# Hybrid recurrent, retention and FFN block: written order for three engines from the retention output to the output projection, and another order of the seven products

## The chip, the cores and the metric

The kernel runs on one core of a Trainium2 chip. TensorE (PE) multiplies, VectorE (DVE) and ScalarE (ACT) work elementwise on SBUF and PSUM, SyncE (SP) issues the loads. The metric is the device time of one execution in microseconds. Before the change it is 1084.58 us, the median of three runs (1083.65 to 1086.42).

## What is computed

One layer over 16 meta and 512 given tokens with 1024 channels. A normed input goes through one wide projection into eight parts: a gated linear recurrence, a retention with four heads of 512 value channels, and two gates. Cut to what the change touches:

```python
z = xn @ w_in[l]
u_rnn, u_gate, q, k, v, g_ret, ga, gb = jnp.split(z, IN_SPLITS, axis=-1)
...
o = retention(q, k, v.reshape(bsz, t, RET_HEADS, RET_DV))
o_b = head_rms(o).reshape(bsz, t, RET_HEADS * RET_DV) * jax.nn.silu(g_ret)

mixed = (jax.nn.sigmoid(ga) * (o_a @ w_branch_rnn[l])
         + jax.nn.sigmoid(gb) * (o_b @ w_branch_ret[l]))
h = h + mixed @ w_out[l]
```

`head_rms` divides each head's output by the root of the mean of its squares. Then come a norm, an up projection with a short convolution and a GELU gate, a down projection and a last norm. All of it is fp32.

## The kernel before

Every fp32 factor is held as two f16 halves. `split` makes them: the hi half by a scaled copy on ScalarE (L91), the lo half, what hi leaves over, on VectorE (L92), which so waits for ScalarE. A product of two such factors is three matmuls (hi hi, hi lo, lo hi; `SPLIT`).

Weights come in units of up to 1 MB, loaded into one of two raw buffers on SP's queue and split into `wt` tiles, of which there are ten. `unit_load` queues a unit's load and the steps that make its tiles; `tick` emits the next step if the tiles of all units from the current one on stay under `ahead[0]`; `get` emits all that is left of a unit.

The gate projections and the product with `w_branch_ret` use a scheme of seven block products instead of eight on 2 x 2 blocks (`fast_products`). The weight side needs the forms B11, B21, B22 and T1 to T4. `fast_steps` makes them in five steps: a tile with B11, a tile with B21 and B22, three sums on VectorE within the raw buffer (L231 to L233), and two tiles with two T forms each. The token side needs A11, A12, A22 and F3, F5, F6, F7. Each product is 12 matmuls of 257 columns (24 for `w_branch_ret`) into a PSUM bank `pa`, `pb` or `pe`. Three products add up in `pa`; between them ScalarE copies what is there into `kept` (twice) and `last` (L784), so the next product into `pa` waits for the copy. VectorE adds the banks and the copies (L801, L805, L812). The gate function then runs on ScalarE (L817), and `finish` uses the result.

The stretch in question, in the order of the code:

- `retention_out(h)`: four blocks of 24 matmuls (L864), each read twice by ScalarE (copy L868, square L870); VectorE adds the squares up (L872). `head_norm` sums over partitions (L879), takes the root (L881, with a load of ScalarE's function table) and the reciprocal (L883); `scale_head` multiplies it in (L917).
- `gated(h)` for the first three heads: two gate units, interleaved with `retention_out(h + 1)`. At the end of a unit the gate multiplies the head's output (L890), `ob_forms` forms differences d and y of it (L900 to L903) and splits four tensors into the `ob` tiles, four hi on ScalarE and four lo on VectorE.
- `values(h)` between the heads: five blocks of up to 24 matmuls (L842, L834), two to a PSUM pair, each split into `v` tiles.
- The mix stage: units with a sigmoid for `ga` and `gb` (`mix_unit`), the branch products (`branch`, `mix_first`), the two gate units of the fourth head, and `mix_products`, which ends in the `mx` tiles (L981, L987). Then the first of four output blocks, `out_proj(0)` (L1123).

Up to the end of the recurrence, the code that stands before this stretch runs in written order on PE, ACT and DVE (`manual_schedule`, closed at L647). From there on the tile framework's scheduler orders each engine's instructions by its own costs and priorities; the code sets only what depends on what.

## Time and profile before

| | |
|---|---|
| runs | 1083.65, 1084.58, 1086.42 us |
| profiled execution | 1084.11 us, span 1082.4 us |
| granted TensorE clock, mean | 0.999 |
| retention stage, with the change's first product | 290 to 437 us |
| mix stage up to the first output block | 437 to 663 us |

A span is the time from the first instruction to the last. In the views, a row of work gives its busy time, and in square brackets, or behind a second bar, the idle time of its engine just before it and what ended that. PEld is TensorE's weight load, which runs beside the matmuls. Matmuls overlap, so the distance from start to start (pitch) of a block says more than its modelled length.

### The profile page before, as it was taken

To read this page: it belongs to the slowest core of one execution; us is meant where nothing else is said; L and a number is where in the kernel's file an instruction comes from. 1 tells how busy PE (TensorE), PEld (TensorE's weight loads), DVE (VectorE), ACT (ScalarE), POOL (GpSimd) and SP (SyncE) were. 2 spreads that over 40 slices of the span, in tenths; PEclk is the share of its full clock that TensorE was granted. 3 is DMA by queue.
4 is the path that set the end of the run, shared out by engine and by line. 5 is a ranking of instruction groups with operands and counts; after the bars stand their busy time and mean duration, and the time that the engine had idled before them with its cause. 6 is when DMAs were issued, how large, how long until landed. Compare 5 with 4: busy or idle time off the path is not lost.

```text
span 1082.4 us, 20933 instructions
## 1 busy us (share of the span) xinstructions
PE 1059.8 (98%) x9026; PEld 856.8 (79%) x9026; DVE 839.8 (78%) x1220; ACT 567.8 (52%) x847; POOL 6.9 (1%) x20
## 2 busy tenths in 40 slices
PE   8999999999999999999999999999999999999997
PEld 5888888875684858888888885588888888888885
DVE  6875699998786969878697775378767776888875
ACT  6568963534564747566454453264544454454442
POOL 2000000000000000000000000000000000000000
PEclk9999999999999999999999999999999999999999
DMA  5423243431211222423333355053232323113322
GB/s 189 142 88 108 79 137 118 156 118 40 78 41 58 100 64 64 127 88 118 103 103 118 117 195 176 2 188 107 96 109 88 116 80 117 41 60 118 117 79 78
DMA packets 105814, 111.48 MB, mean 103 GB/s; under 512 B 3455, under 2 KB 97381, under 8 KB 105722
## 3 DMA queue, kind: packets, MB, share of 16 engines
q1 hardware_dynamic: 105288, 109.75, 30.9%
q8 instruction: 70, 1.15, 0.4%
q10 hardware_dynamic: 146, 0.27, 0.1%
q14 instruction: 22, 0.18, 0.1%
q0 software_dynamic: 288, 0.14, 0.0%
HBM read 108.05 MB, written 2.10 MB: 102 GB/s over the span
## 4 chain that ended last, share of the span: by engine, by line
PE 71%; DVE 17%; ACT 8%; issue 2%; DMA 1%; ACTq 0%; DVEq 0%
PE ps L370 33%; PE P L1251 9%; PE pa L779 7%; DVE wt L92 5%; PE ps L842 4%; PE pm L370 4%; PE ps L1123 3%; PE pe L779 3%; PE ps L383 2%; ACT wt L91 2%; PE pb L779 2%; PE ps L864 1%; DMA raw<-in_w_out 1%; DVE rnn L578 1%; DVE raw L231 1%
## 5 line engine op out<-in xcount | busy, mean ns | idle before, releaser
L370 PEld LDWEIGHTS <-wt 128*128 128x128 f16 x4224 | 410.7, 97 | 63.5 <-DVE t L670 1.4
L92 DVE SCALAR_TENSOR_TENSOR wt<-raw,wt 128x1024 f16<-128x1024 f32 (+2 forms) x270 | 296.6, 1112 | 73.9 <-ACT wt L91 72.0
L91 ACT ACTIVATE wt<-raw 128x1024 f16<-128x1024 f32 (+2 forms) x270 | 256.2, 964 | 163.7 <-PE ps L370 28.3
L779 PEld LDWEIGHTS <-wt 128*128 128x128 f16 x2016 | 195.2, 97 | 37.5 <-issue 10.3
L370 PE MATMUL ps<-x2h,wt 128*128 128x258 f16 x1440 | 218.9, 273 | 0.0
L370 PE MATMUL ps<-xh,wt 128*128 128x257 f16 (+2 forms) x1056 | 163.9, 275 | 1.1 <-DVE t L670 1.1
L370 PE MATMUL ps<-x2l,wt 128*128 128x258 f16 x720 | 137.8, 273 | 0.0
L1208 DVE SCALAR_TENSOR_TENSOR cv<-ps,vt,cv 128x512 f32<-128x512 f32 x96 | 72.0, 750 | 54.4 <-ACT cv L1206 53.1
L370 PE MATMUL ps<-xl,wt 128*128 128x257 f16 (+2 forms) x528 | 102.3, 275 | 0.0
L1251 PE MATMUL P<-wt,act 128*128 128x256 f16 x792 | 88.3, 273 | 0.0
L1251 PEld LDWEIGHTS <-act 128*128 128x128 f16 x792 | 77.4, 98 | 9.1
L842 PE MATMUL ps<-wt,xh 128*128 128x512 f16 x256 | 76.5, 379 | 1.2 <-DVE v L92 1.0
L779 PE MATMUL pa<-xs,wt 128*128 128x257 f16 x576 | 71.6, 273 | 4.7 <-ACT kept L784 4.4
L1206 ACT ACTIVATE cv<-ps,vt,vt 128x512 f32<-128x512 f32 x48 | 37.1, 773 | 57.1 <-PE ps L370 52.4
L370 PE MATMUL pm<-oa,wt 128*128 128x257 f16 x480 | 55.4, 274 | 0.0
L842 PEld LDWEIGHTS <-xh 128*128 128x128 f16 x256 | 24.8, 98 | 30.9 <-issue 2.9
L842 PE MATMUL ps<-wt,xl 128*128 128x512 f16 x128 | 48.5, 379 | 0.0
L779 PE MATMUL pa<-ob,wt 128*128 128x257 f16 x384 | 45.7, 274 | 2.0 <-ACT kept L784 1.4
L1123 PE MATMUL ps<-wt,mx 128*128 128x512 f16 x192 | 44.9, 379 | 1.6 <-ACT mx L91 1.1
L231 DVE TENSOR_TENSOR raw<-raw 128x1024 f32<-128x1024 f32 x35 | 42.7, 1221 | 0.6
L383 PEld LDWEIGHTS <-wt 128*128 128x128 f16 x288 | 28.4, 100 | 7.3 <-issue 1.5
L1123 PEld LDWEIGHTS <-mx 128*128 128x128 f16 x192 | 17.4, 98 | 20.4 <-ACT mx L91 1.6
(255 smaller groups left out, 1283.9 us busy)
## 6 DMA issues: line engine op xcount, KB each, us to landing
raw<-in_w_in SPq DMA_DIRECT2D x41, 1024.0 KB, 4.8
raw<-in_w_up SPq DMA_DIRECT2D x24, 1024.0 KB, 5.0
raw<-in_w_down SPq DMA_DIRECT2D x48, 256.0 KB, 3.8
raw<-in_w_branch_ret SPq DMA_DIRECT2D x16, 512.0 KB, 4.1
raw<-in_w_branch_rnn SPq DMA_DIRECT2D x8, 640.0 KB, 4.4
raw<-in_w_out SPq DMA_DIRECT2D x4, 1024.0 KB, 5.2
xin<-in_x SPq DMA_DIRECT2D x4, 512.0 KB, 5.2
h<-in_x SPq DMA_DIRECT2D x4, 512.0 KB, 5.2
```

The costliest lines, as they stand in the source:

```text
L91: nc.scalar.activation(hi, src, AF.Copy, scale=s)
L92: nc.vector.scalar_tensor_tensor(lo, src, s, hi, op0=ALU.mult, op1=ALU.subtract)
L231: nc.vector.tensor_tensor(pair, pair, rv[:, :, right].rearrange("p (h k) c -> p h k c", h=2), op=ALU.add)
L370: nc.tensor.matmul(ps[:, hf, :n], w(aw, k, col, P), src(ax, k, c0, n), start=k == 0 and (aw, ax) == (0, 0), stop=k == nk - 1 and aw == 1)
L383: nc.tensor.matmul(ps[:, hf, :n], w(aw, k, col, P), src(ax, k, c0, n), start=k == 0 and (aw, ax) == (0, 0), stop=k == KD - 1 and aw == 1)
L578: nc.vector.tensor_tensor_scan(xr, r, t, 0.0, op0=ALU.mult, op1=ALU.add)
L779: nc.tensor.matmul(ps[:, :257], ws[k // 4](wf, aw, k % 4), src(xf_, ax, k), start=first and k == 0 and (aw, ax) == (0, 0), stop=k == last_ ...
L842: nc.tensor.matmul(pb, xf(ax, k, XF + j0, nb), w(aw, k % 4, 0, 512), start=i == 0, stop=i == 23)
L1123: nc.tensor.matmul(ps[:, n], mx[k][:, a, c0:c0 + P], wo[k // 2](aw, k % 2, n * 512, 512), start=j == 0, stop=j == 23)
L1206: nc.scalar.activation(vv_, ps[:, :, 2:258], AF.Identity, scale=vt2[:, 96 + ch:97 + ch], bias=b_ff[:, ch:ch + 1])
L1208: nc.vector.scalar_tensor_tensor(vv_, ps[:, :, j:j + 256], vt2[:, 48 * j + ch:48 * j + ch + 1], vv_, op0=ALU.mult, op1=ALU.add)
L1251: nc.tensor.matmul(pd[:, 256 * tt:256 * tt + 256], t[:, ax, c0 + tt * P:c0 + tt * P + P], w(wf, aw, i), start=q % 6 == 0 and tt == 0 and i ...
```

## The change

From `retention_out(0)` to the end of `out_proj(0)`, PE, ACT and DVE take their instructions in the order in which the code emits them. The seven products run as B11, B21, T2, T3, T1, B22, T4 (before: B11, T3, T2, B21, T1, B22, T4), the tile with T4 and T2 is made ahead of the one with T1 and T3, and `last` is gone: the copy goes into `g1` itself. A weight form is made at the latest when a product asks for it (`form`), tiles are counted one by one (made, less freed, at most ten), and a step is ticked after every product. In the mix stage, the first product of `mix_products` moves ahead of the gate unit's last two, and another piece of work (`fill`: a unit's first product, a branch, or k = 0 to 3 of the first output block) stands between its sixth and its seventh. `out_proj(0)` ends with k = 4, 5, 7, 6, and its PSUM layout changes behind it. No matmul and no elementwise operation is added or left out.

```diff
@@ -232,38 +232,54 @@
-        at = {"B11": (0, 0), "B21": (1, 0), "B22": (1, bc), "T1": (2, 0), "T3": (2, bc), "T4": (3, 0), "T2": (3, bc)}
+        at = {"B11": (0, 0, 1), "B21": (1, 0, 2), "B22": (1, bc, 2), "T4": (2, 0, 4), "T2": (2, bc, 4),
+              "T1": (3, 0, 5), "T3": (3, bc, 5)}
         def form(nm, a, k):
-            i, c0 = at[nm]
+            i, c0, n = at[nm]
+            while emitted.get(u, 0) < n:
+                emit_step()
             return tiles[i][a][:, k, c0:c0 + bc]
+        u = len(loaded) - 1
         wviews.append(form)
-        return [cut(top, left), cut(low, slice(0, 2 * bc)), sums,
-                cut(top, slice(0, 2 * bc)), cut(low, slice(0, 2 * bc))]
+        return [(cut(top, left), True), (cut(low, slice(0, 2 * bc)), True), (sums, False),
+                (cut(low, slice(0, 2 * bc)), True), (cut(top, slice(0, 2 * bc)), True)]
...
     current = [0]
+    emitted, made, freed = {}, {}, {}
+    exact = [False]
...
     def emit_step():
-        u, run = steps[done[0]]
+        u, (run, new) = steps[done[0]]
         while len(loaded) < min(u + 2, len(units)):
...
         run()
+        emitted[u] = emitted.get(u, 0) + 1
+        made[u] = made.get(u, 0) + new
         done[0] += 1
+    def free(u, n=None):
+        freed[u] = made.get(u, 0) if n is None else freed.get(u, 0) + n
...
-    def get(u):
+    def start(u):
         current[0] = max(current[0], u)
...
             queue(unit_load())
+        return wviews[u]
+    def get(u):
+        start(u)
         while done[0] < len(steps) and steps[done[0]][0] <= u:
...
@@ -276,7 +292,10 @@
             u = steps[done[0]][0]
-            if sum(unit_tiles(i) for i in range(current[0], u + 1)) > ahead[0]:
+            if exact[0]:
+                if sum(made.values()) - sum(freed.values()) + steps[done[0]][1][1] > 10:
+                    return
+            elif sum(unit_tiles(i) for i in range(current[0], u + 1)) > ahead[0]:
                 return
...
@@ -783,35 +803,45 @@
-        kept, last = wtile("kept"), wtile("last")
-        g0, g1 = wtile("g0"), wtile("g1")
+        def release():
+            for u in us:
+                free(u, 1)
         h0, h1 = slice(0, 257), slice(257, TQ)
+        kept = wtile("kept")
         pa = bank("pa")
...
         keep(kept[:, h0], pa)
+        release()
+        yield
+        g0 = wtile("g0")
+        pb = bank("pb")
+        product(pb, "B21", "A12", True)
+        nc.vector.tensor_tensor(g0[:, h0], pb[:, :257], kept[:, h0], op=ALU.add)
+        yield
+        product(pa, "T2", "F6")
+        keep(kept[:, h1], pa)
         yield
...
         yield
-        product(pa, "T2", "F6")
-        keep(kept[:, h1], pa)
-        yield
-        pb = bank("pb")
-        product(pb, "B21", "A12", True)
-        nc.vector.tensor_tensor(g0[:, h0], pb[:, :257], kept[:, h0], op=ALU.add)
-        yield
         product(pa, "T1", "F5")
-        keep(last[:, h0], pa)
-        nc.vector.tensor_tensor(g1[:, h1], pe[:, :257], last[:, h0], op=ALU.add)
+        g1 = wtile("g1")
+        keep(g1[:, h0], pa)
+        nc.vector.tensor_tensor(g1[:, h1], pe[:, :257], g1[:, h0], op=ALU.add)
+        release()
         yield
...
         finish(1, g1)
+        release()
+        yield
         product(pe, "T4", "A22")
...
         finish(0, g0)
+        release()
...
@@ -921,22 +953,27 @@
             a = gate_unit(h, i)
-            next(a)
+            advance(a, 1)
             if i == 0:
                 head_norm(h)
-            for _ in range(2):
-                next(a)
-                tick()
+            advance(a, 2)
             next(other)
             scale_head(h, i)
-            for _ in range(2):
-                next(a)
-                tick()
+            advance(a, 2)
             next(other)
-            for _ in a:
-                pass
+            advance(a, 1)
+            rest(a)
         for _ in other:
...
+    def advance(run, n, each=1):
+        for _ in range(n):
+            next(run)
+            tick(each)
+    def rest(run):
+        for _ in run:
+            tick()
...
@@ -947,7 +984,10 @@
     psum_layout(acc=2, bank=4)
-    ahead[0] = 9
+    for u in range(u_v[1][1] + 1):
+        free(u)
+    exact[0] = True
+    order.enter_context(tc.manual_schedule(engines=ORDERED))
     for _ in retention_out(0):
...
@@ -989,11 +1025,13 @@
-        return fast_products(ws, ob_form, func, finish)
+        return fast_products(u_bb[2 * i:2 * i + 2], ob_form, func, finish)
...
         ps = acc("pm")
-        project(ps, get(us.pop(0)), 0, src, HH, nk)
+        u = us.pop(0)
+        project(ps, get(u), 0, src, HH, nk)
+        free(u)
         tick(2)
...
@@ -1003,19 +1041,27 @@
-    def advance(run, n):
-        for _ in range(n):
-            next(run)
-            tick()
-    def rest(run):
-        for _ in run:
-            pass
+    def out_products(i, ks, ps=None, halo=None):
+        first = ps is None
+        if first:
+            ps = acc("ps")
+        c0 = 2 + P * i
+        for n in range(2):
+            for k in ks:
+                w = get(u_out[k // 2])
+                for a, aw in SPLIT:
+                    nc.tensor.matmul(ps[:, n], mx[k][:, a, c0:c0 + P], w(aw, k % 2, n * 512, 512),
+                                     start=first and k == 0 and (a, aw) == (0, 0),
+                                     stop=k == ks[-1] and k > 5 and a == 1)
+                if halo is not None:
+                    halo_part(halo, 4 * n + k // 2, 4 * (k % 2))
+        return ps
...
             run = mix_unit(u_ga, i)
-            next(run)
+            advance(run, 1)
         advance(run, 4)
...
@@ -1033,30 +1079,33 @@
         after = mix_unit(u_ga, i + 1)
-        next(after)
+        advance(after, 1)
         rest(run)
...
-    def gate_b(i):
-        ahead[0] = 10
-        run = mix_unit(u_gb, i)
-        advance(run, 3)
-        ahead[0] = 12
-        advance(run, 2)
+    def gate_b(i, run, fill):
+        if run is None:
+            run = mix_unit(u_gb, i)
+            advance(run, 1)
+        advance(run, 4)
+        product = mix_products(i)
+        advance(product, 1, 2)
         rest(run)
-        for _ in mix_products(i):
-            tick(2)
-        tick()
-        ahead[0] = 10
-    gate_b(0)
-    gate_a(3)
-    gate_b(1)
-    mix_first(7, branch(u_ba, oa_of, NR))
-    gate_b(2)
-    gate_b(3)
+        advance(product, 4, 2)
+        after = fill()
+        rest(product)
+        return after
+    def first_of(us, i):
+        run = mix_unit(us, i)
+        advance(run, 1)
+        return run
+    gate_a(3, gate_b(0, None, lambda: first_of(u_ga, 3)))
+    mix_first(7, gate_b(1, None, lambda: branch(u_ba, oa_of, NR)))
+    first_out = gate_b(3, gate_b(2, None, lambda: first_of(u_gb, 3)), lambda: out_products(0, range(4)))
...
@@ -1110,21 +1158,9 @@
-    psum_layout(bank=2, acc=3)
-    def out_proj(i):
-        ps = acc("ps")
+    def out_proj(i, ps=None):
         halo = halo_start() if i == 1 else None
-        c0 = 2 + P * i
-        for n in range(2):
-            j = 0
-            for k in range(KD):
-                for a, aw in SPLIT:
-                    nc.tensor.matmul(ps[:, n], mx[k][:, a, c0:c0 + P], wo[k // 2](aw, k % 2, n * 512, 512),
-                                     start=j == 0, stop=j == 23)
-                    j += 1
-                if halo is not None:
-                    halo_part(halo, 4 * n + k // 2, 4 * (k % 2))
+        ps = out_products(i, (4, 5, 7, 6), ps) if ps is not None else out_products(i, range(KD), None, halo)
         hv = h2[i].rearrange("p (a b) -> p a b", a=2)
...
@@ -1136,7 +1172,10 @@
-    xns = [out_proj(0)[0]]
+    xns = [out_proj(0, first_out)[0]]
+    order.close()
+    exact[0] = False
+    psum_layout(bank=2, acc=3)
     for i in range(1, 4):
```

Two places show what this does to the engines' orders. The numbers behind the names tell buffers apart.

On ScalarE, at the crossing from the first to the second gate unit of the first head. `g0`, `g1` are gate values, `ob` and `ob11` the split outputs, `kept` the copy that the next unit's third product waits for, `wt` weight tiles. Before:

```order
L91 ACTIVATE wt_3994<-raw_3866 128x512
L91 ACTIVATE wt_4024<-raw_3866 128x1024
L817 ACTIVATE g0_3565<-g0_3565 128x514
L91 ACTIVATE ob11_3754<-or0_3441 128x257
L91 ACTIVATE ob_3757<-or0_3442 128x514
L91 ACTIVATE wt_4085<-raw_3866 128x1024
L784 ACTIVATE kept_3769<-pa_3773 128x257
L91 ACTIVATE ob_3760<-y_3749 128x514
L91 ACTIVATE ob_3763<-d_3748 128x514
L868 ACTIVATE or1_3623<-ps_3821 128x514
```

Of the changed kernel:

```order
L847 ACT_TABLE_LOAD
L847 ACTIVATE g1_3684<-pa_3563 128x257
L847 ACTIVATE g1_3684<-g1_3684 128x257
L91 ACTIVATE wt_3734<-raw_3249 128x1024
L847 ACTIVATE g0_3586<-g0_3586 128x514
L91 ACTIVATE ob11_3758<-or0_3443 128x257
L91 ACTIVATE ob_3761<-or0_3444 128x514
L91 ACTIVATE ob_3764<-y_3753 128x514
L91 ACTIVATE ob_3767<-d_3752 128x514
L804 ACTIVATE kept_3770<-pa_3771 128x257
L91 ACTIVATE wt_3787<-raw_3601 128x1024
```

`kept` stood ahead of the splits of y and d and now stands behind all four splits.

On VectorE, in the first gate unit of the second head, from the sum for `g1` (L805, now L831) to the start of the output forms. Before:

```order
L805 TENSOR_TENSOR g1_4114<-pe_4135,last_4112 128x257
L917 TENSOR_TENSOR or1_3624<-or1_3624,rt_4132 128x514
L92 SCALAR_TENSOR_TENSOR wt_4416<-raw_4348,wt_4416 128x1024
L92 SCALAR_TENSOR_TENSOR wt_4433<-raw_4348,wt_4433 128x1024
L872 TENSOR_TENSOR ssum_4173<-ssum_4173,sq_4263 128x514
L890 TENSOR_TENSOR or1_3622<-g1_4114,or1_3622 128x514
L812 TENSOR_TENSOR g0_4113<-pe_4135,kept_4111 128x257
L92 SCALAR_TENSOR_TENSOR wt_4542<-raw_4414,wt_4542 128x512
L92 SCALAR_TENSOR_TENSOR wt_4572<-raw_4414,wt_4572 128x1024
L890 TENSOR_TENSOR or1_3621<-g0_4113,or1_3621 128x514
L231 TENSOR_TENSOR raw_4414<-raw_4414 128x2x4x128
```

Of the changed kernel:

```order
L831 TENSOR_TENSOR g1_4236<-pe_4208,g1_4236 128x257
L92 SCALAR_TENSOR_TENSOR wt_4241<-raw_4091,wt_4241 128x1024
L904 TENSOR_TENSOR ssum_4178<-ssum_4178,sq_4270 128x514
L922 TENSOR_TENSOR or1_3623<-g1_4236,or1_3623 128x514
L92 SCALAR_TENSOR_TENSOR wt_4288<-raw_4091,wt_4288 128x1024
L841 TENSOR_TENSOR g0_4140<-pe_4208,kept_4116 128x257
L922 TENSOR_TENSOR or1_3622<-g0_4140,or1_3622 128x514
L932 TENSOR_TENSOR d_4306<-or1_3622,or1_3623 128x514
L933 TENSOR_TENSOR y_4307<-or1_3622 128x257
L934 TENSOR_TENSOR y_4307<-d_4306 128x257
```

The sum for `g0` (L812, now L841) came right behind the gate product of `g1`; now the lo half of a weight tile stands between them, and another one ahead of the addition of squares.

More of the change, by code (lines that the diff above doesn't have):

```diff
@@ L206, in run @@
                 split(tiles[i][:, 0, sl], tiles[i][:, 1, sl], raw[:, i * hn:(i + 1) * hn][:, sl], SW)
-            return run
+            return run, c == 0
         wviews.append(lambda a, k, c0, m: tiles[k // hk][:, a, k % hk * ncol + c0:k % hk * ncol + c0 + m])
@@ L457, in first_step @@
     def first_step():
-        steps[done[0]][1]()
+        steps[done[0]][1][0]()
         done[0] += 1
@@ L769, in x_forms, with fast_products @@
         return x_form_t[i // 2][:, 2 * (i % 2) + a, k]
-    def fast_products(ws, src, func, finish):
+    def fast_products(us, src, func, finish):
+        ws = [start(u) for u in us]
         last_k = 4 * len(ws) - 1
@@ L846, in values @@
         vv[h] = vt
+        for u in u_v[h]:
+            free(u)
     def retention_out(h):
@@ L892, in finish @@
                 ob_forms(h, i, ot[2 * i], ot[2 * i + 1])
-        return fast_products([get(u_gr[h][i])], x_forms, gate_func(AF.Silu), finish)
+        return fast_products([u_gr[h][i]], x_forms, gate_func(AF.Silu), finish)
     def ob_forms(h, i, t0, t1):
@@ L970, in mix_unit @@
     def mix_unit(us, i):
-        return fast_products([get(us[i])], x_forms, gate_func(AF.Sigmoid), lambda j, g: sig.update({2 * i + j: g[:, :TQ]}))
+        return fast_products([us[i]], x_forms, gate_func(AF.Sigmoid), lambda j, g: sig.update({2 * i + j: g[:, :TQ]}))
     def mix_products(i):
-        ua, ub = u_bb[2 * i], u_bb[2 * i + 1]
-        ws = [get(ua), get(ub)]
-        current[0] = ua
         def func(dst, src, sign, c0):
@@ L1026, in hybrid_block_kernel @@
         run = gate_unit(3, i)
-        next(run)
+        advance(run, 1)
         if i == 0:
@@ L1039, in hybrid_block_kernel @@
     mix_first(5, branch(u_ba, oa_of, NR))
-    def gate_b(i):
-        ahead[0] = 10
-        run = mix_unit(u_gb, i)
-        advance(run, 3)
-        ahead[0] = 12
-        advance(run, 2)
-        rest(run)
-        for _ in mix_products(i):
-            tick(2)
-        tick()
-        ahead[0] = 10
-    gate_b(0)
-    gate_a(3)
-    gate_b(1)
-    mix_first(7, branch(u_ba, oa_of, NR))
-    gate_b(2)
-    gate_b(3)
+    def gate_b(i, run, fill):
[5 more added lines that the diff above has]
+        advance(product, 1, 2)
+        rest(run)
+        advance(product, 4, 2)
[4 more added lines that the diff above has]
+        run = mix_unit(us, i)
+        advance(run, 1)
+        return run
+    gate_a(3, gate_b(0, None, lambda: first_of(u_ga, 3)))
+    mix_first(7, gate_b(1, None, lambda: branch(u_ba, oa_of, NR)))
+    first_out = gate_b(3, gate_b(2, None, lambda: first_of(u_gb, 3)), lambda: out_products(0, range(4)))
     x2h = xslot([P, KD, TQ], F16, "x2h")
@@ L1073, in hybrid_block_kernel @@
         nc.sync.dma_start(halo_x[a][0:2], meta[NM - 2:NM, sl])
-    wo = [get(u) for u in u_out]
     def halo_start():
```

3 lines of the change are left out of this document (2 added, 1 removed).

## The prediction

> **What bounds the kernel now.** I read the page's busy line first, then the chain that ended last, then the busy time by stage (the change touches about 290 to 663 us and nothing else), then TensorE's waits in that stretch. In the windows the columns are PE, PEld, DVE, ACT, POOL busy us, granted clock, DMA share, GB/s; in the waits, total us, times, longest.
>
> ```profile
> PE 1059.8 (98%) x9026; PEld 856.8 (79%) x9026; DVE 839.8 (78%) x1220; ACT 567.8 (52%) x847; POOL 6.9 (1%) x20
> PE 71%; DVE 17%; ACT 8%; issue 2%; DMA 1%; ACTq 0%; DVEq 0%
> ...
> 290.00:437.00 147.00, 142.46 (x1204) 105.10 (x1201) 119.90 (x178) 87.74 (x151) 0.00 (x0) 1.00 0.23 77
> 437.00:663.00 226.00, 220.87 (x1949) 189.80 (x1947) 177.92 (x238) 120.15 (x180) 0.00 (x0) 1.00 0.40 127
> ...
> PE pa L779 <- ACT kept L784: 5.8, 9, 1.4
> PE ps L1123 <- ACT mx L91: 1.1, 1, 1.1
> PE ps L842 <- DVE v L92: 1.0, 2, 0.5
> PE pa L779 <- ACT last L784: 0.5, 1, 0.5
> PE ps L1123 <- DVE mx L92: 0.5, 1, 0.5
> PE ps L879 <- DVE ssum L872: 0.2, 1, 0.2
> ```
>
> TensorE is the bound, and it hardly waits: 15 waits, 9.1 us, none over 1.4. A block of 12 matmuls has a pitch of 1.33 us and a modelled length of 1.49 (rows below), so each wait costs about 0.16 more than the view books: 9.1 + 15 x 0.16 = **11.5 us**. That is all that the change could win, 1.1% of the run. What it can lose is not bounded in this way: in the retention stage (290 to 437) VectorE is busy 119.9 of 147 us, 82%, and ScalarE 60%. There the queues of the two have little room, so the order in them matters.
>
> **The change part by part.** Work taken out or added: none. TensorE's and VectorE's instructions are the same in number and shape, `last` only becomes part of `g1`. So every microsecond of difference is a stall of TensorE that comes or goes. I put a stall as the lateness of a block's start against the sum of the pitches ahead of it.
>
> The block pitches, and how long the chain at the end of a gate unit takes, stand in the chain of waits and in the timeline about the first unit crossing:
>
> ```profile
> 301.69 1.33 PE pa L779 x12
> 303.02 1.84 PE ps L864 x24
> ...
> 316.66 0.69 DVE L900 TENSOR_TENSOR d<-or,or 128x514 f32<-128x514 f32 x1
> ...
> 317.60 0.42 DVE L902 TENSOR_TENSOR y<-d 128x257 f32<-128x257 f32 x1
> 317.80 0.37 ACT L784 ACTIVATE kept<-pa 128x257 f32<-128x257 f32 x1
> ...
> 318.07 0.62 ACT L91 ACTIVATE ob<-y 128x514 f16<-128x514 f32 x1
> 318.22 1.49 PE L779 MATMUL pa<-xs,wt 128*128 128x257 f16 x12 [0.78 <-ACT kept L784]
> ...
> 318.73 0.63 ACT L91 ACTIVATE ob<-d 128x514 f16<-128x514 f32 x1
> 319.27 0.58 ACT L868 ACTIVATE or<-ps 128x514 f32<-128x514 f32 x1
> ```
>
> T2 adds into the bank that B11 filled, so it waits until `kept` has been read out of it. Now, `kept` runs at 317.80, ahead of the two splits of y and d; the scheduler put it there because y wasn't ready. And 24 matmuls of retention (1.84 us) stand between the B11 and the T2 of the second unit. Both go. In program order `kept` stands behind all four hi splits of the unit before (the rows of ScalarE's order above), and only B21 stands between B11 and T2.
>
> The chain from L841 (the sum behind T4) to T2 then is bare of any choice. Durations:
>
> ```profile
> L890 DVE TENSOR_TENSOR or<-g,or 128x514 f32<-128x514 f32 x16 | 11.0, 688 | 0.0
> L817 ACT ACTIVATE g<-g 128x514 f32<-128x514 f32 x16 | 10.0, 625 | 3.1 <-DVE g L812 2.9
> L812 DVE TENSOR_TENSOR g<-pe,kept 128x257 f32<-128x257 f32 x20 | 8.4, 419 | 0.0
> ```
>
> Sum 0.42 + silu 0.63 + product with the gate 0.60 (next one follows at its pitch, 0.69 less the overlap of 0.09 that 316.66 + 0.61 shows for the rows of that size) and two hand-overs of 0.05 (318.02 to 318.07): 1.75 us to the start of d. From the start of d to the start of `ob<-y`: 318.07 - 316.66 = 1.41; to the next, 0.54 by 318.73 to 319.27; to `kept` another 0.54; from `kept` to T2 0.42 (317.80 to 318.22): 2.91. Together 4.66 us. L841 can begin when T4 has ended, 1.54 after its start, so T2 starts 6.2 us after T4 at the earliest. TensorE has T4, B11 and B21 to fill this, 3 x 1.33 = 4.0. **Bare stall 2.2 us** at each of four crossings: between the two units of the first three heads, and from the third head's second unit to the first mix unit.
>
> L841 is not on time, however, because VectorE now takes it in written order. Behind B22 stand, for the second head's first unit: L831, a wt lo, the addition of squares, the gate product of g1, another wt lo, L841. Their feeders:
>
> ```profile
> L92 DVE SCALAR_TENSOR_TENSOR wt<-raw,wt 128x1024 f16<-128x1024 f32 x86 | 104.5, 1220 | 29.4 <-ACT wt L91 28.8
> L91 ACT ACTIVATE wt<-raw 128x1024 f16<-128x1024 f32 x86 | 90.2, 1054 | 53.9 <-DVE raw L233 11.8 <-PE pm L370 10.6 <-DMA raw<-in_w_out 8.1
> L231 DVE TENSOR_TENSOR raw<-raw 128x1024 f32<-128x1024 f32 x22 | 26.8, 1220 | 0.3
> L233 DVE TENSOR_TENSOR raw<-raw 128x512 f32<-128x512 f32 x22 | 15.1, 688 | 0.4
> L817 ACT ACT_TABLE_LOAD x8 | 10.3, 1283 | 0.1
> L870 ACT ACTIVATE sq<-ps 128x514 f32<-128x514 f32 x12 | 7.1, 594 | 0.0
> L817 ACT ACTIVATE g<-g 128x257 f32<-128x257 f32 x16 | 6.7, 416 | 1.7 <-DVE g L805 1.6
> L817 ACT ACTIVATE g<-pa 128x257 f32<-128x257 f32 x16 | 6.2, 385 | 2.1 <-PE pa L779 2.0
> L92 DVE SCALAR_TENSOR_TENSOR v<-ps,v 128x512 f16<-128x512 f32 x12 | 8.0, 686 | 12.1 <-ACT v L91 12.1
> ```
>
> I walked this unit by hand with these durations from its B11 at 0. B22 starts at 14.45; T4 at 16.05, after L831. ScalarE, in order: square to 16.3, table load 1.28, two silu 0.30 and 0.42 to 18.3, wt hi to 19.3; only then its wt lo, to 20.4 with the overlap, and L841 behind it at 20.4 instead of 17.6. **2.8 us late**, so the stall of that T2 is 2.2 + 2.8 = 5.0. The other three crossings, walked alike, are late by 4.3 (the three sums L231 to L233, 1.22 + 0.69 + 0.69, stand ahead of L841), 3.3 and 2.6: stalls 6.5, 5.5, 4.8. **Four crossings: 21.8.**
>
> Values of the third and fourth head stand behind a second unit's chain. Their second block needs the first block's v lo, and that is behind the ob lows on VectorE: from L841 1.75 to d, then d, y, y, d and ob11 lo 0.61 + 4 x 0.33, three ob lows 3 x 0.60, v lo 0.69 = 6.2. TensorE has T4 1.33 and 24 matmuls, 5.2 us by the first block of this stage; 1.54 + 6.2 - 6.5 = 1.3 bare, 3.7 with the lateness of 2.4 (the sums stand ahead of L841 here too). The fifth block then waits directly for the fourth, which the scheduler had parted with other products: 1.6. **Two heads: 2 x 5.3 = 10.6.** Inside the units the walk gives 6.0 more, the largest 3.1 where B22 of the second head's first unit needs a weight form whose hi stands behind the sums and two PSUM reads. The retention stage thus stalls 38.4; its share now is about 6 of the 11.5.
>
> The mix stage, walked alike: the fourth head's first unit 9.3 (its T1 behind the ob splits 6.2; a wt hi that waits 1.7 for a w_in load of 4.8 us, and holds g1 on ScalarE; 1.3 at T4), its second unit 5.2, three crossings from a mix product to the next unit 1.0 to 1.1 each, 3.2, and 3.4 at the end of the first output block, whose last weight tile has its hi behind the mx hi. **21.1**, where the scheduler's order has the other 5.5. The fills (a B11, a branch, k = 0 to 3 of the first output block) are what keeps these small; I cost them at nothing, since the same matmuls ran before, at another place.
>
> Unseen in the trace is how VectorE behaves in this order. Below, lateness could be nothing: then the bare stalls are left, 4 x 2.2 + 2 x 1.3 + 2 x 1.6 and some 4 at T1 and the output block, 18.6 in all, less 11.5: 1091. Above, all of the walk's lateness could come with more. I take the walk, since its terms are rows. SP's order hardly moves: two loads of h trade places with two of w_out and one w_up goes earlier, worth nothing with a DMA share of 0.40.
>
> Sum: 38.4 + 21.1 - 11.5 = **+48**, on the profiled execution's 1084.1 (span 1082.4), which lies at the median 1084.6: **1132 us**.
>
> **The clock.**
>
> ```profile
> 1074.00:1078.00 4.00, 2.11 (x10) 0.78 (x8) 3.19 (x6) 2.91 (x8) 0.00 (x0) 1.00 0.81 308
> 1078.00:1080.00 2.00, 0.00 (x0) 0.00 (x0) 0.65 (x2) 0.77 (x2) 0.00 (x0) 0.98 0.50 185
> 1080.00:1081.00 1.00, 0.00 (x0) 0.00 (x0) 0.00 (x0) 0.00 (x0) 0.00 (x0) 0.50 0.99 375
> ```
>
> TensorE's last matmul ends at 1074 + 2.11 = 1076.1, and the granted clock goes to half at 1079.9 (0.98 over two us): 3.8 us of idleness are enough to lose it. No gap before this lasts as long, so in the stretch of the change the clock stays 1.00. Five of my stalls (6.5, 5.5, 5.0, 4.8, 6.2) are longer. The Trainium skill, page "TensorE: Matmul & The Clock Gate", section "What's actually happening", states that the clock halves after an idle window of about 3.4 us and comes back after as long a busy one, and that the window runs freely. The 3.8 us above agree; by the page's figure the gaps below would lose at most 1.7 us each, an estimate, in place of the 1.9 of rival 1. What the return costs after a gap inside the kernel no trace here shows.
>
> **Rivals.**
> 1. *The gaps halve the clock.* If the clock returns after as long a stretch as it took to go, half of 3.8 us is lost at a gap, 1.9; from half of the five gaps to all of them that is 5 to 9.5 us: 1137 to 1142. For it: the row at 1080. Against it: the gaps would have to be as long as I walk them.
> 2. *Only the bare chains stall.* VectorE, which idles during each stall, catches up and L841 is never late: 1090 to 1106. Against it: the wt lo ahead of L841 waits for ScalarE, not for VectorE's own backlog.
> 3. *Faster.* The fills take the waits of the mix and output stage away (5.5), and the crossings cost no more than now: 1084.1 - 5.5 = 1078.6. It holds if `kept` gets out of ScalarE within 2.7 us of B11's start, the two products in between. Against it: 4.66 us of chain ahead of it, against 1.54 less than 4.0 of cover.
> 4. *No change:* the scheduler's order was as near to program order as makes no difference, 1081 to 1087. The rows of the order speak against it.
>
> **How the numbers follow.** Forecast, 1106 to 1138 about the walk: 55%. Clock rival: 22%. Bare chains: 14%. No change: 4%. Faster: 5%. The predicted time is the walk's, 1132. The range reaches down to 1100, into the bare case, and up to 1148, the clock's price on a walk that is a few us short: left out are some 8% bare below 1100, the 4 and the 5, and 3 above. A measurement of this kernel tells about 0.3%, 3.3 us, from no change. By that bound: faster 5%, same 4%, slower 91%.
>
> **What would show it.** TensorE's wait for `kept` grows from 5.8 us to 20 to 35, with a longest of 5 to 7; its wait for v lo grows from 1.0 to about 10 with four to six entries, and a wait for the g1 copy appears. The busy totals of DVE (839.8) and ACT stay within 5 us, and TensorE's work without stalls too. The stage from 290 grows from 147 to about 180, the mix stage from 226 to about 242. Dips of the granted clock below 1.00 in these stages speak for rival 1; waits for `kept` of at most 2.5 for rival 2. I am wrong at the root if `kept`'s wait stays near 1 us: then the order within ScalarE didn't matter, or its neighbours finish sooner than rows of before say.

## The result, and the profile after

The changed kernel takes 1156.75 us, the median of five runs (1154.6 to 1159.12), against 1084.58: a ratio of **1.067**, 95% interval 1.0648 to 1.0691. The forecast was 1132, its range 1100 to 1148.

The busy line and the engines of the chain that ended last, from the page of the changed kernel:

```profile
PE 1078.8 (94%) x9026; PEld 865.0 (75%) x9026; DVE 847.4 (74%) x1220; ACT 564.5 (49%) x847; POOL 6.9 (1%) x20
PE 68%; DVE 18%; ACT 10%; issue 2%; DMA 2%; DVEq 0%; ACTq 0%; SPq 0%
```

TensorE is busy 19.0 us longer with the same 9026 matmuls. TensorE's waits in the changed kernel (total us, times, longest), without those that before had elsewhere too (one of the five for v, 0.2 us, lies ahead of the stretch):

```profile
PE pa L799 <- ACT kept L804: 38.8, 11, 6.4
PE ps L872 <- DVE v L92: 9.3, 5, 3.5
PE pa L799 <- ACT g L804: 4.5, 2, 3.1
PE ps L1054 <- ACT wt L91: 3.9, 1, 3.9
PE pe L799 <- DVE g L831: 2.6, 2, 1.5
...
PE ps L1054 <- DVE wt L92: 0.9, 1, 0.9
...
PE ps L911 <- DVE ssum L904: 0.7, 1, 0.7
```

In the stretch of the change these are 22 waits, 60.5 us, and with 0.16 each, as the prediction counts them, 64.0: 52.5 more than the 11.5 of before.

The stages begin with the first retention matmul and with the first branch matmul, and end with the first output block. Windows with these borders (us, then PE, PEld, DVE, ACT, POOL busy, granted clock, DMA share, GB/s), first before, then after:

```profile
290.00:431.90 141.90, 138.26 (x1167) 101.57 (x1164) 114.80 (x169) 85.52 (x146) 0.00 (x0) 1.00 0.22 73
431.90:668.40 236.50, 230.47 (x2010) 195.72 (x2008) 183.62 (x248) 122.38 (x185) 0.00 (x0) 1.00 0.41 131
```

```profile
287.80:475.50 187.70, 153.19 (x1188) 109.40 (x1185) 132.03 (x187) 94.56 (x156) 0.00 (x0) 0.91 0.20 66
475.50:738.80 263.30, 237.17 (x1985) 198.16 (x1984) 182.42 (x237) 117.50 (x180) 0.00 (x0) 0.95 0.35 113
```

The gate stage is 45.8 us longer, the mix stage 26.8, together 72.6: TensorE idles for 60.6 us where it idled for 9.7, and is busy for 390.4 where it was busy for 368.7. In both stages the clock is below 1.00, where it was full before. The border between the two shifts with the order: two products, 24 matmuls of 0.11 us, which TensorE did behind the first branch matmul before, now stand ahead of it. For equal work the gate stage is some 43 us longer and the mix stage some 29.

The first crossing in the timeline of the changed kernel:

```profile
312.40 1.05 ACT L91 ACTIVATE wt<-raw 128x1024 f16<-128x1024 f32 x1
...
313.48 1.23 DVE L92 SCALAR_TENSOR_TENSOR wt<-raw,wt 128x1024 f16<-128x1024 f32 x1 [0.25 <-ACT wt L91]
314.62 0.42 DVE L841 TENSOR_TENSOR g<-pe,kept 128x257 f32<-128x257 f32 x1
...
318.41 0.62 ACT L91 ACTIVATE ob<-d 128x514 f16<-128x514 f32 x1
318.93 0.37 ACT L804 ACTIVATE kept<-pa 128x257 f32<-128x257 f32 x1
...
319.35 1.02 PE L799 MATMUL pa<-xs,wt 128*128 128x257 f16 x4 [6.39 <-ACT kept L804]
```

The sum for g0 starts behind a weight split; 4.73 us later, behind four splits and `kept`, T2 starts. The prediction's chain had 4.66. TensorE stood for 6.39 us, and then ran at half clock, as windows of 3.41 us about this gap show:

```profile
310.17:313.58 3.41, 2.79 (x26) 2.31 (x24) 2.01 (x4) 3.25 (x5) 0.00 (x0) 1.00 0.02 5
313.58:316.99 3.41, 0.00 (x0) 0.00 (x0) 2.68 (x4) 1.15 (x3) 0.00 (x0) 1.00 0.24 50
316.99:320.40 3.41, 1.05 (x6) 0.73 (x6) 3.38 (x9) 2.95 (x6) 0.00 (x0) 0.50 0.67 257
320.40:323.81 3.41, 3.41 (x21) 2.52 (x20) 2.97 (x5) 2.12 (x3) 0.00 (x0) 0.50 0.00 0
323.81:327.22 3.41, 3.41 (x37) 3.02 (x35) 2.17 (x4) 2.03 (x3) 0.00 (x0) 1.00 0.88 296
```

21 matmuls start in a window at half clock where the next one has 37. The trace of the changed kernel has twelve such spells of half clock in the two stages, seven of 3.41 us and five of 6.83. 216 matmuls start in them, at about twice their pitch (0.214 us for 0.110 at 257 columns, 0.427 for 0.216 at 512): some 22 us. The busy time of the two stages grew by 21.6, of which 1.1 is the tail of seven more blocks that end in a wait (0.16 each), so by that measure the spells cost 20 to 21.

### The profile page after: what moved, and what is told of

It is laid out like the page before. It is cut to its first block, busy times and chain, and to the rows that moved or that the text cites. A ratio compares the mean times of both kernels' runs of the same rounds, so it can differ in the third digit from the quotient of the medians.

```text
span 1152.8 us, 20889 instructions
## 1 busy us (share of the span) xinstructions
PE 1078.8 (94%) x9026; PEld 865.0 (75%) x9026; DVE 847.4 (74%) x1220; ACT 564.5 (49%) x847; POOL 6.9 (1%) x20
## 4 chain that ended last, share of the span: by engine, by line
PE 68%; DVE 18%; ACT 10%; issue 2%; DMA 2%; DVEq 0%; ACTq 0%; SPq 0%
PE ps L389 32%; PE P L1290 9%; PE pa L799 7%; PE ps L872 5%; DVE wt L92 4%; PE pm L389 3%; PE ps L1054 3%; ACT wt L91 3%; PE pe L799 2%; PE ps L402 2%; PE ps L896 2%; DMA raw<-in_w_in 2%; DVE raw L231 1%; ACT g L847 1%; DVE raw L233 1%
## 5 line engine op out<-in xcount | busy, mean ns | idle before, releaser
L389 PEld LDWEIGHTS <-wt 128*128 128x128 f16 x4224 | 411.7, 97 | 65.2 <-DVE t L689 1.7
L91 ACT ACTIVATE wt<-raw 128x1024 f16<-128x1024 f32 (+2 forms) x270 | 253.3, 961 | 155.3 <-DVE raw L233 60.6
L799 PEld LDWEIGHTS <-wt 128*128 128x128 f16 x2016 | 202.0, 101 | 83.1 <-issue 49.8
L799 PE MATMUL pa<-xs,wt 128*128 128x257 f16 x576 | 81.6, 297 | 43.4 <-ACT kept L804 38.8
L92 DVE SCALAR_TENSOR_TENSOR v<-ps,v 128x512 f16<-128x512 f32 x20 | 13.6, 687 | 40.1 <-ACT v L91 40.1
L91 ACT ACTIVATE v<-ps 128x512 f16<-128x512 f32 x20 | 11.6, 592 | 53.0 <-PE ps L872 52.6
```

What stands on the lines that cost most here:

```text
L91: nc.scalar.activation(hi, src, AF.Copy, scale=s)
L92: nc.vector.scalar_tensor_tensor(lo, src, s, hi, op0=ALU.mult, op1=ALU.subtract)
L389: nc.tensor.matmul(ps[:, hf, :n], w(aw, k, col, P), src(ax, k, c0, n), start=k == 0 and (aw, ax) == (0, 0), stop=k == nk - 1 and aw == 1)
L799: nc.tensor.matmul(ps[:, :257], ws[k // 4](wf, aw, k % 4), src(xf_, ax, k), start=first and k == 0 and (aw, ax) == (0, 0), stop=k == last_ ...
```

## The experiments

All times are medians beside runs of the kernel before on the same chip; stage lengths are taken by the borders above.

**Is it the order at all, and do the stages add up?** `e1_scheduler` drops the one line that makes the order the written one (the diff's removed line); `e4_gated_only` keeps it and closes the written order at the first mix unit (the added line); `e5_mix_only` drops it and opens the written order at that place.

```diff
-    order.enter_context(tc.manual_schedule(engines=ORDERED))
     for _ in retention_out(0):
...
+    order.close()
     gate_a(0)
```

> The changed kernel with the scheduler ordering the three engines again from the retention output on; the new order of the seven products, the forms on demand, the tile count and the fills stay. Theory A (the written order alone costs the 72 us): 1080 to 1092 us, and the stalls of TensorE from 288 us to the end of the first output block under 20 us, the granted clock at 1.00 throughout. Theory B (the other order of the products, or weight tiles that come later by the exact count, cost it): over 1120 us.

> Written order only from the retention output to the end of the third head's gate; the scheduler orders the mix stage and the output block. Theory A (the losses of the two stages add up as the stalls and the half clock of each show them: 38.4 + 12.4 less the 7.5 of before in this one): 1122 to 1133 us. Theory B (the mix stage's losses come out of what the gate stage leaves late): under 1110 or over 1145 us.

> Written order on the three engines only from the first mix unit to the end of the first output block; the scheduler orders the gate stage. Theory A (each stage loses what its own stalls and half clock show: 28.6 + 10.1 less the 9.0 of before in this one, and 38 us in e4_gated_only, together the 72 of the change): 1110 to 1120 us. Theory B (the stages' losses depend on each other through the weight tiles): under 1104 or over 1125 us.

Measured: e1 1085.89 us, ratio 1.0006 (0.999 to 1.0021), no difference to be measured: together, the other order of products, the forms on demand, the exact count and the fills cost nothing and win nothing under the scheduler. The clock is not at 1.00 throughout, as A had it: one spell of 3.41 us stands at the end of the output block. e4 1122.54 (1.0352, 1.0337 to 1.0368), e5 1112.75 (1.0269, 1.0239 to 1.0299): 37.9 and 28.7 us over their own runs of before, together 66.6 of the 72. All three times lie in A's range. Most of the rest belongs to the fourth crossing, from the third head's gate to the first mix unit, where the border lies: TensorE waits 4.70 us for `kept` there in the changed kernel, with a spell of half clock behind it, and 0.64 in e4 and 0.78 in e5.

**What does the half clock cost?** `e3_fillers` adds matmuls of no use ahead of the twelve longest waits.

```diff
+    def fill_up(n):
+        t = bank("fill")
+        for _ in range(n):
+            nc.tensor.matmul(t[:, :257], xf(0, 0, XF, P), xf(0, 0, XF, 257), start=True, stop=True)
```

> The changed kernel with matmuls of no use into a spare PSUM bank ahead of the twelve longest waits (14 to 46 of 257 columns at 0.11 us each, all but 1.3 to 1.6 us of each wait of the changed kernel); the waits themselves stay. Theory A (half clock after a gap costs what the matmuls' longer pitch shows, 22 us): the clock stays at 1.00 and the time is 1132 to 1142 us. Theory B (the slower pitch is not of the gaps' making, or the fillers push the work behind them back): 1150 us or more.

Measured: 1140.45 us, 16.3 less than the changed kernel, though TensorE has 308 matmuls more. Its windows over the two stages:

```profile
291.10:470.60 179.50, 163.06 (x1379) 123.08 (x1375) 131.17 (x187) 93.75 (x157) 0.00 (x0) 0.99 0.21 67
470.60:724.80 254.20, 240.88 (x2105) 205.41 (x2104) 182.11 (x238) 117.07 (x180) 0.00 (x0) 1.00 0.36 116
```

One spell of 3.41 us is left of twelve. A holds: idleness alone made TensorE slower. The rest of the 22 us is that spell, some 1.7, and longer waiting: no filler outlasted its wait (0.16 to 2.4 us of each is left), but idle time (433.7 less 403.9, 29.8) and fillers (308 at 0.11, 33.9) are together some 3 us more than the 60.6 of the changed kernel.

**What does T2 wait for at a crossing?** `e2_kept_first` emits the next unit's first product and copy ahead of the silu and the output forms, `e7_two_copies_first` its first three products and both copies.

```diff
         nc.vector.tensor_tensor(g0[:, h1], pe[:, :257], kept[:, h1], op=ALU.add)
+        if us[0] in LATE:
+            yield
         func(g0[:, :TQ], g0[:, :TQ], 1.0, 0)
         finish(0, g0)
...
-            advance(a, 1)
+            next(a)
+            if i == 1:
+                rest(before)
+            tick()
```

> One part of the written order undone: at four crossings (unit 0 to 1 of the first three heads, third head to first mix unit) the next unit's first product and its copy into kept are emitted ahead of the last silu and the output forms of the unit before; all else as in the changed kernel. Theory A (kept behind the four splits is what T2 waits for): the four waits of 6.4, 3.6, 5.4 and 4.7 us go, and with them four or five spells of half clock worth some 9 us; a few us come back later since silu starts 1 to 2 us later: 1125 to 1137 us. Theory B (T2 waits for something else that is late at the same time, such as the weight form or VectorE): over 1148 us.

> As e2_kept_first, but at the four crossings the next unit's first three products and both of their copies into kept are emitted ahead of the last silu and the output forms of the unit before. Theory A (in e2 the wait only moved to the second copy, which still stood behind the forms): both waits go at the crossings, 20.7 us of stalls and some 9 us of half clock, and up to 6 us come back at other places: 1126 to 1136 us. Theory B (the crossings wait for an amount of work on VectorE and ScalarE, not for its order): 1146 us or more.

Measured: e2 1151.98 us (ratio 1.0624, 1.0607 to 1.0641), e7 1144.01 (1.0548, 1.0519 to 1.0577). Neither time is in A's range; e2's is in B's, e7's between the two. A's mechanism shows at the crossing itself, its sum doesn't. The first crossing in e2's timeline:

```profile
313.47 1.49 PE L801 MATMUL pa<-xs,wt 128*128 128x257 f16 x12 [0.81 <-ACT kept L806]
320.94 1.45 PE L801 MATMUL pa<-xs,wt 128*128 128x257 f16 x6 [2.79 <-ACT kept L806]
```

T2 waits 0.81 instead of 6.39; T1 then waits 2.79, for the second copy, which stands behind the forms and two weight splits. In e7 no wait for `kept` is left at the four crossings but the 0.81 of the first, and the gate stage has shrunk from 187.7 to 172.5 us. But new waits of 1.0 to 2.2 us stand at B22 and T4 there (for the g1 copy and for L831), the fourth head's wait for v grew from 3.5 to 4.6, and the fourth head's first unit waits 4.0 us for `kept` where it waited 0.1, because its weights come later:

```profile
474.97 1.58 ACT L91 ACTIVATE wt<-raw 128x512 f16<-128x512 f32 x2 [5.14 <-DMA raw<-in_w_in]
...
481.30 0.37 ACT L806 ACTIVATE kept<-pa 128x257 f32<-128x257 f32 x1
```

What is put off at one place is late at another: in the stretch TensorE waits for 58.2 us in e2 and 52.6 in e7, for 60.5 in the changed kernel.

**Is weight work what makes the sum for g0 late, and can it go?** `e8_ticks_behind` moves the steps ticked after T1 and B22 behind the output forms.

```diff
             scale_head(h, i)
-            advance(a, 2)
+            advance(a, 1)
+            next(a)
             next(other)
-            advance(a, 1)
+            next(a)
             rest(a)
+            tick(2)
```

> The changed kernel with the weight steps that are ticked after T1 and after B22 of the first three heads' gate units emitted behind the output forms instead, so that no weight split stands between the sums for g1 and g0 on VectorE. Theory A (the wait at a crossing is a bare chain of 2.2 us and the rest is lateness of the sum for g0 behind weight work): the stalls of 6.6, 3.8, 5.5 and 4.9 us fall to 2 to 4.5 each, and with them values and three spells of half clock: 1136 to 1148 us. Theory B (the weight work is needed there, and its products now wait for it): 1153 us or more.

Measured: 1161.08 us, slower than the change itself and in B's range. The third head's crossing in e8:

```profile
449.07 0.42 DVE L841 TENSOR_TENSOR g<-pe,kept 128x257 f32<-128x257 f32 x1
...
454.81 1.22 DVE L231 TENSOR_TENSOR raw<-raw 128x1024 f32<-128x1024 f32 x1
...
457.52 1.06 ACT L91 ACTIVATE wt<-raw 128x1024 f16<-128x1024 f32 x1 [4.05 <-DVE raw L233]
458.48 0.37 ACT L804 ACTIVATE kept<-pa 128x257 f32<-128x257 f32 x1
...
458.90 1.45 PE L799 MATMUL pa<-xs,wt 128*128 128x257 f16 x6 [8.34 <-ACT kept L804]
```

The mechanism is neither theory's as written. ScalarE was idle for 4.05 us ahead of the weight hi at 457.52, with the forms done, but in written order that split now stands ahead of `kept`, and it waits for the three sums, which VectorE does behind its ob lows. The first and fourth crossings did shrink (to 5.1 and 3.1); the second grew from 3.6 to 4.2 and this one from 5.4 to 8.3.

**What do the values wait for, and does cover help?** `e9_two_pairs` puts the first two blocks into two PSUM pairs. `e13_retention_first` emits the 1.84 us of retention ahead of T2 (the diff's second piece).

```diff
-            if b % 2 == 0:
-                ps = acc("ps")
-            pb = ps[:, b % 2]
+            if b in (0, 1, 4):
+                pairs.append(acc("ps"))
+            pb = pairs[2][:, 0] if b == 4 else pairs[b % 2][:, b // 2]
...
-            advance(a, 2)
-            next(other)
+            advance(a, 1)
+            next(other)
+            advance(a, 1)
```

> The changed kernel with the first two blocks of values in two PSUM pairs instead of one (third and fourth block in their second halves). Theory A (the second block waits only because the first block's lo split reads the same PSUM pair): the waits for v of 2.8, 1.4, 3.5 and 1.4 us go, and two spells of half clock behind them, 8 matmuls of 0.43 instead of 0.21 each: 1142 to 1149 us. Theory B (the work in front on ScalarE and VectorE holds TensorE up at the next place): 1153 us or more.

> The changed kernel, written order on all three engines, with the retention block emitted ahead of T2 in the gate units of the first three heads. Theory A (the wait at the crossing ends at a fixed time after T4, so 1.84 us of cover take 1.84 us off it, at three of the four): 1144 to 1153 us. Theory B (the retention block's PSUM copies and squares enter the queues earlier and hold up what follows): 1155 us or more.

Measured: e9 1142.64 us, 14.1 less than the change, and no wait for v is left. e13 1152.27, 4.5 less: its waits at the three crossings are 4.55, 2.29 and 3.55 for 6.39, 3.59 and 5.38, shorter by 1.84, 1.30 and 1.83, and it comes back in longer waits at other places (for v 11.4 for 9.3). Both times lie in A's range. In e13 that is in part for another reason than A's: the waits in the stretch are 60.0 us in all for 60.5, and what its profiled execution gains is half clock, nine spells of 37.5 us together for twelve of 58.0.

**Which engine's order is it?** `e6_pe_only`, `e10_act_only` and `e14_dve_only` keep the written order on one engine each.

```diff
-    order.enter_context(tc.manual_schedule(engines=ORDERED))
+    order.enter_context(tc.manual_schedule(engines={mybir.EngineType.PE}))
```

> Written order on TensorE alone; ScalarE and VectorE are ordered by the scheduler in the same stretch. Theory A (the loss sits in the queues of ScalarE and VectorE, where the copy stands behind work that isn't ready): 1082 to 1098 us, no wait of TensorE over 2 us. Theory B (TensorE's own order costs it, since only one product of 1.33 us is left between the first product and the one that needs its copy): 1115 us or more, with waits for kept of 2 us and more at the crossings.

> Written order on ScalarE alone from the retention output to the first output block; TensorE and VectorE are the scheduler's. Theory A (the queue that holds the copies is what TensorE waits for, so ScalarE's order alone carries most of the 50 us that TensorE's own order, 23 us, leaves over): 1112 us or more. Theory B (VectorE's order, by the lateness of the sum for g0, carries it): under 1098 us.

> Written order on VectorE alone in the same stretch; TensorE and ScalarE are the scheduler's. Theory A (ScalarE's queue carries it): 1083 to 1100 us. Theory B (VectorE's order does): 1110 us or more.

Measured, with the length of the two stages:

| written order on | us | ratio (95%) | gate stage | mix stage | matmuls ahead of the border | both at equal work |
|---|---|---|---|---|---|---|
| none (before) | 1084.58 | 1 | 141.9 | 236.5 | 1160 | 141.9, 236.5 |
| TensorE | 1107.03 | 1.0207 (1.0188 to 1.0226) | 166.6 | 233.5 | 1184 | 164.0, 236.1 |
| ScalarE | 1105.55 | 1.0203 (1.0181 to 1.0225) | 145.4 | 252.4 | 1124 | 149.4, 248.4 |
| VectorE | 1120.92 | 1.0344 (1.0322 to 1.0366) | 150.5 | 265.5 | 1136 | 153.1, 262.9 |
| all three | 1156.75 | 1.067 (1.0648 to 1.0691) | 187.7 | 263.3 | 1184 | 185.1, 265.9 |

The last column is an estimate: it moves the matmuls by which a run differs from before over the border, at 0.11 us each.

Each expectation was an either-or. e6 and e10 fell between their two theories; e14 lies in the range of B, VectorE's order. But no engine carries it alone: each one's order costs by itself, 2.0 to 3.4%. In the gate stage TensorE's order costs most, in the mix stage VectorE's, and there TensorE's own order costs nothing. TensorE's waits in e6:

```profile
PE pa L799 <- ACT kept L804: 11.8, 7, 3.3
PE ps L872 <- DVE v L92: 10.5, 4, 3.8
```

At its four crossings TensorE waits 2.2, 3.3, 2.0 and 1.8. That this is about the bare stall of 2.2 is chance, since the chain is another one: at all four the scheduler has `kept` ahead of the splits of y and d again. With VectorE's order alone the longest wait is at the end of the output block, for the lo half of a weight tile; the two largest totals in e14:

```profile
PE pa L799 <- ACT kept L804: 11.5, 11, 3.7
PE ps L1054 <- DVE wt L92: 7.4, 1, 7.4
```

**Is a faster version to be had?** `e11_pe_mix`: written order on TensorE alone, from the first mix unit on. `e12_pe_pairs_ret`: e6 with the edits of e9 and e13. `e15_old_gates_pe_mix`: e11 with the old order of products and tiles for the first three heads.

> Written order on TensorE alone, and only from the first mix unit to the end of the first output block; all else is the scheduler's. Theory A (in the mix stage the written order with its fills is good for TensorE, and only ScalarE's and VectorE's queues spoiled it; in e6_pe_only this stage took 233.5 us where before it took 236.4): 1079 to 1083 us, 1 to 4 us faster than before. Theory B (nothing is to be had there): 1084 us or more.

> e6_pe_only with the values' first two blocks in two PSUM pairs, and with the retention block of 1.84 us emitted ahead of T2 instead of behind it in the gate units of the first three heads. Theory A (TensorE's written order loses 23 us by uncovered waits: 11.1 us for v, 10.0 at four crossings, and the half clock behind them): the waits for v go, three crossings shrink by 1.84 each: 1081 to 1091 us. Theory B (the loss has another source): 1097 us or more.

> As e11_pe_mix (written order on TensorE alone in the mix stage), with the first three heads' gate units in the old order of products and weight tiles. Theory A (the old order covers the copy in the gate stage, 141.9 us before against 145.8 in e11; the mix stage keeps its 233): 1080 to 1083 us, faster than before by 1 to 4 us. Theory B (the gate stage's 4 us are of the exact tile count, not of the product order): 1085 to 1088 us.

Measured: e11 1086.43 us (ratio 1.0019, 1.0008 to 1.003), e12 1089.37 (1.0053, 1.0037 to 1.0069), e15 1088.74 (1.0034, 1.002 to 1.0049). e11 lies in B's range and e15 above both of its ranges; e12 lies in A's range and confirms what e6 lost: 18 us come back when v and the crossings are covered. None beats the kernel before.

The hope behind e11 and e15 was an artefact of the border. Their mix stages (e11 233.2, e12 232.2, e15 233.8, for 236.5) look 3 to 4 us shorter and their gate stages (145.8, 150.1, 148.3, for 141.9) longer, but as in e6 the written order puts 24 matmuls, 2.6 us, ahead of the border that the scheduler has behind it. The two stages together, which no border shifts, are 379.0, 382.3 and 382.1 for 378.4. So the 4 us of the gate stage, which e15 was to explain by the product order or the exact count, are for the most part moved work. Of what is left, the wait at the fourth crossing is the largest piece that the traces show: 1.75, 3.33 and 2.98 us for 0.90 before, in e12 and e15 with a spell of half clock behind it.

## Why the prediction was wrong, step by step

- **The bound held.** TensorE was the bound, and there was little to win: with the change's parts under the scheduler nothing was won (e1).
- **The bare chain held:** 4.66 us forecast, 4.73 measured at the first crossing, where the cover was 4.0.
- **The lateness held in sum.** Stalls at the crossings (waits plus 0.16): forecast 6.5, 5.0, 5.5, 4.8, measured 6.6, 3.8, 5.5, 4.9. Values: 10.6 forecast, 9.8 measured. Inside the units: 6.0 and 5.8. Gate stage together 38.4 forecast, 36.2 measured. But lateness isn't a thing to be lifted out alone, as the prediction's sum of terms suggests: e2, e7 and e8 moved it, and it came back in part, nearly whole, or with more added (52.6, 58.2 and 67.6 us of waits in e7, e2 and e8, for 60.5), at other instructions of the same queues.
- **The mix stage was mis-sized:** 21.1 forecast, 27.8 measured. The fourth head's units are right (9.3 and 5.2 forecast, 9.1 and 4.7 measured). The term "three crossings from a mix product to the next unit 1.0 to 1.1 each, 3.2" measured 8.9 in four waits, and the end of the output block 5.1 for 3.4. I gave VectorE no weight work ahead of the sum there. The third of these crossings in the changed kernel:

```profile
655.97 1.22 DVE L231 TENSOR_TENSOR raw<-raw 128x1024 f32<-128x1024 f32 x1
...
658.55 0.42 DVE L841 TENSOR_TENSOR g<-pe,kept 128x257 f32<-128x257 f32 x1
...
660.46 0.63 ACT L91 ACTIVATE mx<-m 128x514 f16<-128x514 f32 x1 [5.14 <-DVE m L1023]
661.00 0.37 ACT L804 ACTIVATE kept<-pa 128x257 f32<-128x257 f32 x1
...
661.42 0.96 PE L799 MATMUL pa<-xs,wt 128*128 128x257 f16 x5 [2.98 <-ACT kept L804]
```

  The three sums stand ahead of L841, and `kept` behind the mx split that waits for L841's chain: the gate stage's mechanism once more.
- **The step that failed** is the sentence "Five of my stalls are longer", with the price of rival 1, "5 to 9.5 us", beside a forecast without it. The row at 1080 was read as a threshold, under which a gap costs nothing. The runs show no such threshold. A gap of 2.8 us already halved the clock (the wait for v that ends at 339.98, with half clock from 340.89), so twelve spells came instead of at most five. They cost 20 to 22 us, 1.7 to 1.8 each on average. That this comes near the prediction's 1.9 for one is partly luck: by half of TensorE's busy time in them, the short spells cost up to 1.7 us and the five long ones 2.1 to 2.9. Of the miss of 24.7 us, 4.5 are waits (52.5 for 48) and the other 20 the half clock. And what I kept as a rival at 22% followed from my own forecast: whoever forecasts five gaps of 4.8 us and more, with a row that halves the clock after 3.8, has the half clock in the forecast. The sign that it named, busy totals that stay within 5 us, failed where it counts: TensorE's grew by 19.0. VectorE's grew by 7.6 as well, but there the lengths of the instructions add up to the same (909.2 us before, 907.6 after); fewer of them overlap the one before.
- **The other rivals fell:** no bare-chain case (waits for `kept` up to 6.4), and no gain from the fills, neither under the scheduler (e1) nor with TensorE alone in written order (e11).

## What to carry to other kernels

A written order over three engines that feed each other can put the copy which frees an accumulator behind work that isn't ready, as it did here; look at what stands ahead of each such copy, on each engine, and at how much TensorE work lies between the product and its successor. To move one such instruction may mend little, since its delay can pass to the next one in the same queue. And a forecast of gaps of 3 us or more on TensorE has to carry the half clock after them, as a term of the sum. When stages of two orders are compared, count the work on each side of the border first: here two products that crossed it looked like a gain of 3 us.

## What the runs showed of the hardware

That so short a gap halves the clock was new to me, and the traces show by what rule. The spells begin and end on a grid of 3.41 us: in all seventeen profiles, every change of the granted clock lies a whole number of such windows from the first one. Two windows of the grid in the changed kernel, with those after them:

```profile
501.31:504.72 3.41, 1.49 (x12) 1.17 (x12) 2.79 (x6) 2.09 (x4) 0.00 (x0) 1.00 0.49 143
504.72:508.13 3.41, 3.31 (x30) 2.92 (x30) 3.34 (x5) 1.98 (x3) 0.00 (x0) 1.00 0.00 0
...
692.46:695.87 3.41, 1.28 (x12) 0.97 (x10) 2.64 (x5) 0.93 (x2) 0.00 (x0) 1.00 0.31 82
695.87:699.28 3.41, 2.44 (x12) 1.73 (x12) 3.41 (x5) 2.39 (x4) 0.00 (x0) 0.50 0.79 251
699.28:702.70 3.42, 3.42 (x18) 2.39 (x17) 2.83 (x5) 0.39 (x1) 0.00 (x0) 0.50 0.71 285
702.70:706.10 3.40, 3.40 (x33) 2.98 (x32) 1.24 (x2) 2.25 (x4) 0.00 (x0) 1.00 0.00 1
```

A window in which TensorE is busy for 1.28 us (0.38) is followed by half clock; one with 1.49 (0.44) isn't. At half clock, a window with 2.44 (0.72) is followed by another one, a full one by full clock. Over sixteen profiles, the changed kernel's and those of the fifteen experiments, every full-clock window with a busy share under 0.39 was followed by half clock and none over 0.47, while in between both happened; every half-clock window up to 0.76 by another and none from 0.77 on. The Trainium skill, page "TensorE: Matmul & The Clock Gate", section "What's actually happening", has the free-running window and its length, and these runs agree; it asks for an idle window, and here one that was idle for about 60% of its length did. Worked out from these shares, a gap of 4.2 us costs wherever it falls on the grid (twice 0.61 x 3.41), one of 1.8 us or less (0.53 x 3.41) doesn't by itself, and what lies between depends on where it falls: an estimate, for a TensorE that is otherwise busy. Short gaps add up within a window: two of 0.9 us, at the end of e1's output block (658.41 to 661.83, busy share 0.47), did cost a spell.
